# Second mixer of a two-layer decoder trunk: one transpose for both diagonal blocks of a triangular inverse, and five elementwise steps on other engines

## The chip, the cores and the metric

The kernel runs on one core of a Trainium2 chip. The core has TensorE (matmuls, written PE in the profile), VectorE (DVE), ScalarE (ACT), GpSimd (POOL), and SyncE (SP), which here only issues transfers. The metric is the device time of one execution in microseconds; a kernel's time is the median over its runs.

## What is computed

The reference is a trunk of two layers on a sequence of 512 tokens of width 1024. Each layer is a half feed-forward block, a token mixer, and another half feed-forward block, each followed by a layer norm:

```python
x = layer_norm(alpha * x + 0.5 * swiglu_ffn(x, ffn1_wi[l], ffn1_wo[l]), ...)
mix = even_mixer(x, ...) if l % 2 == 0 else odd_mixer(x, ...)
x = layer_norm(alpha * x + mix, ...)
x = layer_norm(alpha * x + 0.5 * swiglu_ffn(x, ffn2_wi[l], ffn2_wo[l]), ...)
```

The change touches the mixer of the second layer, `odd_mixer`. It runs two groups of heads side by side: RWKV-7 (8 heads of 64) and gated linear attention (GLA, 4 heads). The RWKV-7 part is a recurrence over time on a 64 x 64 state per head:

```python
def step(state, inp):
    r_t, w_t, k_t, v_t, kk_t, a_t = inp
    sa = jnp.einsum('bhij,bhj->bhi', state, -kk_t)
    state = (state * w_t[:, :, None, :] + sa[..., None] * (kk_t * a_t)[:, :, None, :]
             + v_t[..., None] * k_t[:, :, None, :])
    return state, jnp.einsum('bhij,bhj->bhi', state, r_t)
...
k = k * (1.0 + (a - 1.0) * k_a)
bonus = (jnp.sum(r * k * r_k, -1, keepdims=True) * v).reshape(B, S, RK_WIDTH)
return (y + bonus) * g
```

The GLA part ends in `head_norm(o, norm_g, None, GLA_NORM_EPS) * jax.nn.silu(og)`.

## The kernel before

All matrix products with weights are made as three matmuls each, from a high and a low part of both operands (lines 122, 123 and 126 for outputs with features on the partitions, 146 to 148 and 155 to 157 for outputs with tokens there). ScalarE makes the high part of each weight tile (line 98, `whi`), VectorE the low part (line 100, `wlo`).

In the second mixer, `odd` (line 555), the recurrence is cut into 8 chunks of 64 tokens. The 512 RWKV-7 channels are four feature tiles `ft` of 128 partitions, two heads each, and two tiles make a group, so there are two groups, each with 2 x 2 x 8 = 32 blocks of 64 x 64 (head and chunk). For each tile:

- `inputs(ft)` projects k, r and v and shifts them in time (line 599 on ScalarE, line 600 on VectorE).
- `keys(ft, ...)` (line 675) makes the decayed keys. Line 707 forms `fa = tha * KA + KAI` on VectorE, line 708 multiplies it by k, line 709 makes the decayed r, line 711 uses `fa`. Line 714 then overwrites r with r * RK * fa. Line 697 is a power on GpSimd for the norms of the keys.
- `bonus` (line 727) multiplies that r by a block of ones (line 729, `pb`).
- `scores` (line 733) makes two halves of four chunks each: matmuls of keys into `psc` (line 742), and the masked copy to `SC` on VectorE (line 744). Columns 64 to 127 of `SC`, rows 0 to 63, hold for each block a strictly upper triangular 64 x 64 matrix: two diagonal blocks of 32 x 32 (rows 0 to 31 with columns 64 to 95, rows 32 to 63 with columns 96 to 127), an upper block, and a lower block which is zero.
- `natural` (line 746) makes token-major copies.

`inverse(grp)` (line 770) inverts the two 32 x 32 diagonal blocks of all 32 matrices at once on VectorE. Line 778 transposes each diagonal block into `X`, one instruction on 32 partitions for each. Then 30 steps of two instructions each (lines 782 and 783, on 64 partitions) do the substitution, line 784 sets the diagonal, line 786 transposes the upper one of the results into `TQ`, which lies in the tile `WT`, and line 789 transposes both results back into `SC`, again one instruction for each block. `merge(grp)` (line 791) makes the off-diagonal block with matmuls: `pq` (line 800) needs line 786, its copies are line 802 (one half on ScalarE, one on VectorE); `px` (line 807) needs those and the lower right block of `SC`; its copies into `SC` are line 809; `pwt` and `pu` (line 822) read all of rows 0 to 63, columns 64 to 127. `chain(grp)` (line 830) then walks through the chunks.

The order at the top of the mixer is: `keys` and `scores` of the first group, its `inverse`, `gla_gates`, `natural`, `merge`; `keys` of tiles 2 and 3; `chain` of the first group; `scores`, `natural` and `inverse` of the second; its `merge` and `chain`. Line 917 to 959 and `gla` are the GLA part; in `gla_o`, line 957 to 959 make the gated output `og` (line 959 multiplies by the norm's weights, `ng`), which line 1030 reads much later.

Two things set the order of instructions. TensorE's waits are filled with projection work: `fill()` (line 646) puts as many steps of a waiting projection at its place as the list `FILL` (line 25, written out by hand) says, and ties them behind the last matmul before them. All else is ordered by a planner when the kernel is built: it simulates a timeline with its own estimate of each instruction's cost, and on each engine issues what is ready, in the order that comes out. So if instructions change engine, the planned order can change too, also that of instructions which the edit does not name.

Of the kernel before, what the change touches and what calls it, by code (L numbers as in the profile page):

```python
# [10 lines left out]
AF = mybir.ActivationFunctionType  # L11
ALU = mybir.AluOpType
# [19 lines left out]
class Net:  # L32
# [522 lines left out]
    def odd(self, l):  # L555
# [7 lines left out]
        with tc.tile_pool(name="od", bufs=1) as ep:  # L563
# [11 lines left out]
            IMU, KAI = 43, 56  # L575
# [17 lines left out]
            def col(i, n=P):  # L593
                return pc[:n, i:i + 1]
# [80 lines left out]
            def keys(ft, Dm, k, r, v):  # L675
# [30 lines left out]
                fa = slot("wk")  # L706
                V.tensor_scalar(out=fa, in0=tha, scalar1=col(KA + ft), scalar2=col(KAI + ft), op0=ALU.mult, op1=ALU.add)
                V.tensor_tensor(out=fa, in0=fa, in1=k, op=ALU.mult)
# [4 lines left out]

                V.scalar_tensor_tensor(out=r, in0=r, scalar=col(RK + ft), in1=fa, op0=ALU.mult, op1=ALU.mult)
                fill()
# [17 lines left out]
            def scores(f, grp, KRV, bk):  # L733
                KV, BK, SC, ZU, WT, R, _ = grp

                for c0 in (0, 4):
# [6 lines left out]
                    for par, p in enumerate(pp):  # L743
                        V.tensor_tensor(out=SC[:, 2 * f + par, c0:c0 + 4, :], in0=p.rearrange("p (c t) -> p c t", c=4), in1=m_rk.unsqueeze(1).broadcast_to([P, 4, P]), op=ALU.mult)

            def natural(f, grp, KRV, bk):
                KV, BK, SC, ZU, WT, R, _ = grp
# [22 lines left out]
            def inverse(grp):  # L770
# [4 lines left out]
                tmp = ZU[64:128].rearrange("p h c t -> p (h c t)")[:, 1024:1280]  # L775
                for z in range(2):
                    q = slice(32 * z, 32 * z + 32)
                    V.transpose(out=X[q], in_=SM[q, :, 64 + 32 * z:96 + 32 * z].rearrange("p m t -> p t m"))
                for j in range(1, 31):
# [6 lines left out]
                V.transpose(out=TQ[0:32].rearrange("p m j -> p j m"), in_=X[0:32].rearrange("p t j -> p j t"))  # L786
                for z in (1, 0):
                    q = slice(32 * z, 32 * z + 32)
                    V.transpose(out=SM[q, :, 64 + 32 * z:96 + 32 * z].rearrange("p m t -> p t m"), in_=X[q])

# [160 lines left out]
            def gla_o():  # L951
# [3 lines left out]
                for t in range(4):  # L955
                    o = gp.tile([P, S], F32, name=f"og{t}")
                    A.activation(o, acc[t], AF.Tanh, scale=0.5)
                    V.scalar_tensor_tensor(out=o, in0=o, scalar=1.0, in1=acc[t], op0=ALU.add, op1=ALU.mult)
                    V.tensor_tensor(out=o, in0=o, in1=ng, op=ALU.mult)
                    og.append(o)  # L960
# [304 lines left out]
```

## Time and profile before

| | |
|---|---|
| median of 3 runs | 2059.55 us (2056.95 to 2061.2) |
| the profiled execution | 2057.05 us, of which the span from first to last instruction is 2055.3 us |
| mean granted TensorE clock | 0.983 |
| VectorE busy | 1002.1 us, 1858 instructions |
| ScalarE busy | 687.5 us, 1206 instructions |
| GpSimd busy | 68.5 us, 128 instructions |
| the second mixer | about 1340 to 1660 us after the span's start |
| the two inverses, line 778 to line 789 | 1411.15 to 1468.40 and 1534.99 to 1576.99 |

How to read the profile's lines. In a timeline a line is: start and duration in us, engine, source line, operation, tile written <- tiles read, shape written <- shape read (partitions x elements per partition), how many instructions the line merges, and in brackets the idle time of that engine just before and who ended it. In a table of groups, a line is: source line, engine, operation, tiles, shapes and count, then total busy us and mean ns of one instruction, then the idle time before them and what ended it. In a table by stage, a line is the stage's start and end, its length, then each engine's busy time with its number of instructions, the granted TensorE clock as a share of full speed, the share in which the transfer engines were busy, and GB/s.

### The profile page before, as it was taken

Reading aid. Unit: us, or ns where it says so; the run is one execution under the profiler, and the core shown is the slowest. Engines: PE = TensorE matmul, PEld = TensorE weight load, DVE = VectorE, ACT = ScalarE, POOL = GpSimd, SP = SyncE. Lnnn points to the kernel's source line nnn. Section 1 sums busy time; section 2 is a strip of 40 time slices with the busy share of each in tenths; the row PEclk is TensorE's granted clock in tenths of the full one; section 3 lists DMA queues with packets and bytes.
Section 4 is the critical chain, followed back from the end, with each engine's and each line's share of the span. In section 5 each row is a group of like instructions: output and inputs, shape, how many; then the busy total and the mean of one; then the engine's idle time right before and its main releaser. Section 6 shows DMA issues by size and latency. Waiting matters only on the chain.

```text
span 2055.3 us, 26008 instructions
## 1 busy us (share of the span) xinstructions
PE 2014.7 (98%) x10485; PEld 1670.5 (81%) x10485; DVE 1002.1 (49%) x1858; ACT 687.5 (33%) x1206; POOL 68.5 (3%) x128
## 2 busy tenths in 40 slices
PE   9999999999999999999999999998898999999998
PEld 8888888977888888888888888886777688888886
DVE  4332333766783323336332333678758684323335
ACT  4331331556423322332332233255223334322330
POOL 0000000100010000000000000000010210000001
PEclk9999999999999999999999999998898999999999
DMA  5233332322233233332333333241113023333331
GB/s 176 93 102 113 103 93 82 107 92 62 66 100 113 92 102 114 101 95 72 113 92 103 113 98 97 86 140 40 59 31 114 1 74 119 95 97 118 94 102 62
DMA packets 56456, 191.42 MB, mean 93 GB/s; under 512 B 7488, under 2 KB 7952, under 8 KB 56336
## 3 DMA queue, kind: packets, MB, share of 16 engines
q1 hardware_dynamic: 56336, 189.77, 29.4%
q8 instruction: 82, 1.34, 0.3%
q14 instruction: 38, 0.31, 0.0%
HBM read 185.55 MB, written 4.19 MB: 92 GB/s over the span
## 4 chain that ended last, share of the span: by engine, by line
PE 90%; DVE 7%; ACT 1%; DMA 1%; issue 1%; POOL 0%; POOLq 0%; DVEq 0%; SPq 0%; ACTq 0%
PE pgu L122 16%; PE pgu L123 16%; PE pgu L126 16%; PE acc L157 8%; PE acc L155 8%; PE acc L156 8%; PE pout L155 1%; PE pout L156 1%; PE pout L157 1%; DVE wlo L100 1%; PE pj L122 1%; PE pj L123 1%; PE pj L126 1%; PE pst L168 1%; DVE ZU L782 1%; DVE ZU L783 1%
## 5 line engine op out<-in xcount | busy, mean ns | idle before, releaser
L100 DVE TENSOR_TENSOR wlo<-raw,whi 128x512 fp32r<-128x512 f32 x658 | 426.4, 686 | 549.6 <-ACT whi L98 513.2
L98 ACT ACTIVATE whi<-raw 128x512 fp32r<-128x512 f32 x661 | 379.6, 623 | 841.8 <-PE pgu L123 401.2
L122 PE MATMUL pgu<-xh,whi 128*128 128x512 f32 (+1 forms) x1568 | 563.1, 368 | 1.5 <-ACT whi L98 1.3
L123 PE MATMUL pgu<-xl,whi 128*128 128x512 f32 (+1 forms) x1568 | 564.0, 368 | 0.0
L126 PE MATMUL pgu<-xh,wlo 128*128 128x512 f32 (+1 forms) x1568 | 353.6, 367 | 0.0
L122 PEld LDWEIGHTS pgu<-xh,whi 128*128 128x128 f32 x1568 | 294.1, 188 | 50.4 <-ACT whi L98 1.5
L123 PEld LDWEIGHTS pgu<-xl,whi 128*128 128x128 f32 x1568 | 295.3, 189 | 48.6
L126 PEld LDWEIGHTS pgu<-xh,wlo 128*128 128x128 f32 x1568 | 275.8, 189 | 48.6
L155 PE MATMUL acc<-whi,hh 128*128 128x512 f32 x704 | 274.4, 390 | 0.0
L156 PE MATMUL acc<-whi,hl 128*128 128x512 f32 x704 | 274.2, 389 | 0.0
L157 PE MATMUL acc<-wlo,hh 128*128 128x512 f32 x704 | 272.3, 390 | 0.0
L233 DVE TENSOR_TENSOR sg<-sg,pgu 128x512 f32<-128x512 f32 (+1 forms) x96 | 61.6, 642 | 334.2 <-PE pgu L126 330.5
L156 PEld LDWEIGHTS acc<-whi,hl 128*128 128x128 f32 x704 | 132.2, 188 | 27.3
L157 PEld LDWEIGHTS acc<-wlo,hh 128*128 128x128 f32 x704 | 132.2, 188 | 27.2
L155 PEld LDWEIGHTS acc<-whi,hh 128*128 128x128 f32 x704 | 132.2, 188 | 27.0
L160 ACT ACTIVATE hh<-sg 128x512 fp32r<-128x512 f32 (+1 forms) x96 | 57.3, 597 | 120.9 <-DVE sg L233 120.9
L232 ACT ACTIVATE sg<-pgu 128x512 f32<-128x512 f32 (+1 forms) x96 | 53.7, 561 | 55.6 <-PE pgu L126 54.9
L160 ACT ACTIVATE xh<-pst 128x512 fp32r<-128x512 f32 x48 | 27.6, 598 | 108.5 <-PE pst L168 108.5
L122 PE MATMUL pj<-xh,whi 128*128 128x512 f32 (+2 forms) x184 | 63.5, 364 | 0.0
L190 POOL TENSOR_SCALAR rs<-mv 128x1 f32<-128x1 f32 x24 | 13.1, 547 | 1507.8 <-DVE mv L188 1507.8
L123 PE MATMUL pj<-xl,whi 128*128 128x512 f32 (+2 forms) x184 | 62.0, 354 | 0.0
L161 DVE TENSOR_TENSOR hl<-sg,hh 128x512 fp32r<-128x512 f32 (+1 forms) x96 | 61.5, 640 | 0.6 <-ACT hh L160 0.5
(336 smaller groups left out, 1968.6 us busy)
## 6 DMA issues: line engine op xcount, KB each, us to landing
raw<-ffn_wi SPq DMA_DIRECT2D x176, 512.0 KB, 3.5
raw<-ffn_wo SPq DMA_DIRECT2D x88, 512.0 KB, 3.5
raw<-od_krv SPq DMA_DIRECT2D x12, 512.0 KB, 3.5
raw<-ev_qk SPq DMA_DIRECT2D x8, 512.0 KB, 3.6
raw<-ev_rg SPq DMA_DIRECT2D x8, 512.0 KB, 3.5
raw<-ev_w_out SPq DMA_DIRECT2D x8, 512.0 KB, 3.5
raw<-od_w_out SPq DMA_DIRECT2D x8, 512.0 KB, 3.5
x<-x SPq DMA_DIRECT2D x4, 512.0 KB, 5.7
```

Source lines behind the costliest of these rows:

```text
L98: self.nc.scalar.activation(hi[:, sl], t[:, sl], AF.Copy)
L100: self.nc.vector.tensor_tensor(out=lo[:, sl], in0=t[:, sl], in1=hi[:, sl].bitcast(F32), op=ALU.subtract)
L122: mm(o, hi[:, kt, :n], self.xh[:, kt, t0:t1], start=kt == 0, stop=False)
L123: mm(o, hi[:, kt, :n], self.xl[:, kt, t0:t1], start=False, stop=lo is None and kt == 7)
L126: mm(o, lo[:, kt, :n], self.xh[:, kt, t0:t1], start=False, stop=kt == 7)
L155: mm(o, ah, hi[:, cs], start=first and i == 0, stop=False)
L156: mm(o, al, hi[:, cs], start=False, stop=False)
L157: mm(o, ah, lo[:, cs], start=False, stop=last and i == len(lhs) - 1)
L160: self.nc.scalar.activation(hi, src, AF.Copy)
L161: self.nc.vector.tensor_tensor(out=lo, in0=src, in1=hi.bitcast(F32), op=ALU.subtract)
L232: nc.scalar.activation(sg, pp[f, 0][:, t0:t1], AF.Silu)
L233: nc.vector.tensor_tensor(out=sg, in0=sg, in1=pp[u][:, t0:t1], op=ALU.mult)
```

## The change

The lower left 32 x 32 block of each matrix in `SC`, which is zero, serves as a place to put the lower right diagonal block under the upper left one, so that both stand in columns 64 to 95 of partitions 0 to 63. For this ScalarE copies the lower right block over in `scores`, after line 744. One transpose on 64 partitions then replaces the two of line 778, and one replaces the two of line 789. After that ScalarE copies the lower right result back to its own columns, and GpSimd sets the borrowed block to zero again.

Besides, `fa` of line 707 is made on ScalarE; line 714 becomes a scaling on ScalarE followed by a multiply on GpSimd; and the multiply of line 959 goes to GpSimd. `FILL` stays as it is.

```diff
@@ keys
                 fa = slot("wk")
-                V.tensor_scalar(out=fa, in0=tha, scalar1=col(KA + ft), scalar2=col(KAI + ft), op0=ALU.mult, op1=ALU.add)
+                A.activation(fa, tha, AF.Identity, scale=col(KA + ft), bias=col(KAI + ft))
                 V.tensor_tensor(out=fa, in0=fa, in1=k, op=ALU.mult)
...
-                V.scalar_tensor_tensor(out=r, in0=r, scalar=col(RK + ft), in1=fa, op0=ALU.mult, op1=ALU.mult)
+                A.activation(r, r, AF.Copy, scale=col(RK + ft))
+                G.tensor_tensor(out=r, in0=r, in1=fa, op=ALU.mult)
@@ scores
                         V.tensor_tensor(out=SC[:, 2 * f + par, c0:c0 + 4, :], ...)
+
+                    s = SC[32:64, 2 * f:2 * f + 2, c0:c0 + 4, :]
+                    A.activation(s[:, :, :, 64:96], s[:, :, :, 96:128], AF.Copy)
@@ inverse
-                for z in range(2):
-                    q = slice(32 * z, 32 * z + 32)
-                    V.transpose(out=X[q], in_=SM[q, :, 64 + 32 * z:96 + 32 * z].rearrange("p m t -> p t m"))
+                V.transpose(out=X, in_=SM[0:64, :, 64:96].rearrange("p m t -> p t m"))
...
                 V.transpose(out=TQ[0:32].rearrange("p m j -> p j m"), in_=X[0:32].rearrange("p t j -> p j t"))
-                for z in (1, 0):
-                    q = slice(32 * z, 32 * z + 32)
-                    V.transpose(out=SM[q, :, 64 + 32 * z:96 + 32 * z].rearrange("p m t -> p t m"), in_=X[q])
+                V.transpose(out=SM[0:64, :, 64:96].rearrange("p m t -> p t m"), in_=X)
+                A.activation(SM[32:64, :, 96:128], SM[32:64, :, 64:96], AF.Copy)
+                G.memset(SM[32:64, :, 64:96], 0.0)
@@ gla_o
-                    V.tensor_tensor(out=o, in0=o, in1=ng, op=ALU.mult)
+                    G.tensor_tensor(out=o, in0=o, in1=ng, op=ALU.mult)
```

## The prediction

> **What bounds the kernel now.** I read the page first: engine totals, then the chain that ended last.
>
> ```profile
> PE 2014.7 (98%) x10485; PEld 1670.5 (81%) x10485; DVE 1002.1 (49%) x1858; ACT 687.5 (33%) x1206; POOL 68.5 (3%) x128
> PE 90%; DVE 7%; ACT 1%; DMA 1%; issue 1%; POOL 0%; POOLq 0%; DVEq 0%; SPq 0%; ACTq 0%
> ```
>
> TensorE sets the end nearly everywhere; VectorE owns 7% of the chain. An edit that takes work from VectorE can pay only where TensorE waits for VectorE. So I cut the second mixer into stages (busy time per engine; the figure behind POOL's is the granted TensorE clock) and asked who waits longest for whom.
>
> ```profile
> core 0: us, PE busy (x) PEld busy (x) DVE busy (x) ACT busy (x) POOL busy (x), PEclk, DMA share, GB/s
> 1391.00:1431.00 40.00, 33.14 (x181) 22.22 (x179) 35.12 (x61) 23.24 (x37) 2.96 (x5) 0.86 0.12 40
> 1431.00:1463.00 32.00, 32.00 (x168) 26.17 (x166) 29.21 (x67) 11.68 (x20) 1.11 (x1) 0.96 0.26 76
> 1463.00:1485.00 22.00, 16.54 (x283) 13.73 (x282) 13.57 (x16) 5.20 (x9) 0.53 (x1) 0.69 0.15 48
> ...
> 1568.00:1588.00 20.00, 12.88 (x180) 10.01 (x180) 12.75 (x16) 3.64 (x7) 0.00 (x0) 0.66 0.15 55
> ```
> ```profile
> PE pq L800 <- DVE WT L786: 6.2, 2, 4.8
> ```
>
> Two ends of an inverse stand out. At the first (1463 to 1485) TensorE is idle 22.00 - 16.54 = 5.46 us, at the second (1568 to 1588) 20.00 - 12.88 = 7.12 us; the longest wait of the kernel is TensorE's for L786, the transpose that ends the inverse. Both stages also show a clock of 0.69 and 0.66. In rows of 2 us the clock is full or about half (one with 0.51 stands further down), so a mean of 0.69 is half clock for 22 x 0.31 / 0.5 = 13.6 us, and 0.66 for 20 x 0.34 / 0.5 = 13.6 us. Between them, 1431 to 1463, TensorE has no gap: there a quicker VectorE buys nothing by itself. From 1391 to 1431 TensorE is idle 6.86 us in small waits.
>
> The timeline of VectorE around the two inverses:
>
> ```profile
> 1391.47 1.29 DVE L100 TENSOR_TENSOR wlo<-raw,whi 128x512 fp32r<-128x512 f32 x2 [5.03 <-PE pj L126]
> ...
> 1417.07 0.75 DVE L714 SCALAR_TENSOR_TENSOR kr<-kr,pc,wk 128x512 f32<-128x512 f32 x1
> ...
> 1434.37 0.43 DVE L966 TENSOR_SCALAR cst<-cst 128x512 f32<-128x512 f32 x1 [0.92 <-DMA cst<-gla_norm_g]
> ...
> 1462.47 1.98 DVE L786 STREAM_TRANSPOSE WT<-ZU 32x1024 f32<-32x1024 f32 x1
> 1464.49 3.92 DVE L789 STREAM_TRANSPOSE SC<-ZU 32x1024 f32<-32x1024 f32 x2
> ...
> 1469.22 0.69 DVE L802 COPY WT<-pq 32x512 f32<-32x512 f32 x1
> ...
> 1474.27 0.69 DVE L809 COPY SC<-px 32x512 f32<-32x512 f32 x1
> ...
> 1571.28 1.90 DVE L786 STREAM_TRANSPOSE WT<-ZU 32x1024 f32<-32x1024 f32 x1
> 1573.20 3.79 DVE L789 STREAM_TRANSPOSE SC<-ZU 32x1024 f32<-32x1024 f32 x2
> 1577.02 0.69 DVE L802 COPY WT<-pq 32x512 f32<-32x512 f32 x1
> ```
>
> and TensorE's matmuls that stood behind it (in brackets: how long, and for whom):
>
> ```profile
> 1395.33 1.33 PE L908 MATMUL pl<-ga,gw 80*128 80x512 f32 x2 [1.86 <-DVE wk L721]
> ...
> 1422.27 1.02 PE L729 MATMUL pb<-kr,cst 128*128 128x512 f32 x2
> ...
> 1464.60 1.20 PE L800 MATMUL pq<-WT,SC 32*32 32x32 f32 x64 [1.37 <-DVE WT L786]
> ...
> 1475.01 1.76 PE L822 MATMUL pwt<-SC,KV 64*64 64x64 f32 x28 [2.70 <-DVE SC L809]
> ...
> 1573.32 1.81 PE L800 MATMUL pq<-WT,SC 32*32 32x32 f32 x64 [4.79 <-DVE WT L786]
> ...
> 1577.77 1.91 PE L807 MATMUL px<-SC,WT 32*32 32x32 f32 x62 [1.66 <-DVE WT L802]
> ```
>
> The reading: after L786 the two L789 transposes hold up the copy L802, which px needs, and in the first merge a queue of other VectorE work holds up L809, which pwt needs.
>
> **The change, part by part.** Durations of what is moved, with ScalarE's rows for the same shapes:
>
> ```profile
> L778 DVE STREAM_TRANSPOSE ZU<-SC 32x1024 f32<-32x1024 f32 x4 | 7.9, 1986 | 0.1
> L714 DVE SCALAR_TENSOR_TENSOR kr<-kr,pc,wk 128x512 f32<-128x512 f32 x4 | 3.0, 747 | 0.1
> L959 DVE TENSOR_TENSOR og<-og,cst 128x512 f32<-128x512 f32 x4 | 2.8, 689 | 0.1
> L707 DVE TENSOR_SCALAR wk<-wk,pc 128x512 f32<-128x512 f32 x4 | 2.1, 536 | 0.0
> ```
> ```profile
> L599 ACT ACTIVATE kr<-pj,pc 128x512 f32<-128x512 f32 x12 | 8.1, 681 | 3.9 <-PE pj L126 3.9
> L802 ACT COPY WT<-pq 32x512 f32<-32x512 f32 x2 | 1.2, 577 | 7.3 <-PE pq L800 7.3
> ```
>
> *Transposes.* Four L778 become two on 64 partitions, four L789 likewise. No row shows a 64-partition transpose. Its ends are the time of one 32-partition transpose (1.99 us) and of two (3.97 us). I take 1.99: each partition still carries 1024 elements. So 2.0 us go ahead of each inverse and 1.9 us behind it. In exchange ScalarE gets eight mask copies of 256 elements (at most the 0.58 us of the 512-element copy) and two copies of 1024 elements (about twice 0.58, 1.15 us), and GpSimd two memsets.
>
> *Elementwise.* L707 (4 x 0.54 us) goes to ScalarE at about 0.68 each (L599's form). L714 (4 x 0.75 us) becomes a ScalarE scaling (0.68) and a GpSimd multiply. L959 (4 x 0.69 us) becomes a GpSimd multiply. In all VectorE loses 3.97 + 3.8 + 2.1 + 3.0 + 2.8 = 15.7 us; what of it lies on the path is the question.
>
> *GpSimd's price.* The nearest rows, and two that show how GpSimd and VectorE meet:
>
> ```profile
> L697 POOL TENSOR_TENSOR nrm<-nrm,expo 128x8 f32<-128x8 f32 x4 | 6.7, 1681 | 73.5 <-DVE nrm L696 73.5
> ...
> L329 POOL MEMSET wbd<- 128x1024 f32 x1 | 1.0, 956 | 4.4 <-DVE x L196 4.4
> ```
> ```profile
> 1408.57 0.75 POOL L932 COPY Dg<-E 128x8 f32<-128x8 f32 x1 [3.12 <-ACT E L930]
> 1410.13 0.19 POOL L932 COPY Dg<-E 128x8 f32<-128x8 f32 x1 [0.81 <-ACT E L930]
> ```
> ```profile
> 1408.12 1.21 DVE L920 TENSOR_TENSOR_SCAN ga<-cst,wk 128x512 f32<-128x512 f32 x1
> ```
>
> A multiply of 512 elements lies between half the 1024-element memset (0.48) and the longest row of this stage (1.68); I take 1.1, the middle. The same GpSimd copy took 0.19 us, but 0.75 us when VectorE's scan was running, and ended with it (1409.32 against 1409.33). So GpSimd waits out a VectorE instruction that reads two tensors from SBUF. The Trainium skill, "SBUF — State Buffer", section "SBUF: two separate sides", says that the two share a port pair as an exclusive lock, and that a GpSimd instruction which reads SBUF likewise keeps such a VectorE instruction out for its whole length. The trace agrees with the first half; no row here can show the second, since GpSimd's reads are tiny. I therefore charge each GpSimd multiply in a stretch where VectorE is packed with between 0 and 1.1 us of VectorE time, and take 1.1: there the move loses 0.4 us instead of winning 0.7. The skill's "GPSIMD Engine Reference", section "Performance versus the Vector engine", gives 4497 ns for a two-input operation on 2048 elements, from which I estimate 1.12 us here; by that figure the sum would be unchanged. The memset (about 1.0 us) runs behind the ScalarE copy while px and its copies run; if these didn't cover it, it would cost pwt up to 1.0 us.
>
> *First pair of keys.* For ft 0 and 1 the moved steps lie before 1391, where VectorE then sits idle 5.03 us waiting for TensorE: nothing gained.
>
> *First inverse.* Between L778 and L786 there go one transpose (2.0), L714 twice (1.5) and L707 once (0.54), 4.0 us; the two GpSimd multiplies give back 2.2. L786 ends 1.9 us earlier, and pq's 1.37 us are gone. Behind it 1.96 us of L789 go too, so L809 comes 1.9 + 1.96 = 3.9 us earlier. TensorE's 5.46 idle us there shrink by **3.9**; with no lock by all 5.46. What is late next: TensorE's own packed matmuls before 1463.
>
> *Clock at the first inverse.* Of 13.6 us at half clock TensorE is busy about 10.2 (all but 0.7 and 2.70), so full clock would be worth 5.1. About 1.5 us of idle remain. In this trace an idle 1.86 us (L908) was followed by half clock, shown by the row below, but only for some 4 us. So I take **2.0** of the 5.1; ends 0 and 5.1.
>
> ```profile
> 1396.00:1398.00 2.00, 2.00 (x5) 1.61 (x6) 1.77 (x3) 2.00 (x4) 0.00 (x0) 0.51 0.00 0
> ```
>
> *Second inverse.* Ahead of L786: 2.0 us of transpose, less 0.5 for the last mask copy, which now stands between L744 and the transpose, and 0.7 for the L959 that ran just before L786: pq starts **2.2** earlier, 2.6 of the 4.79 stay. Then px started 4.45 us after pq, behind two L789. Now the transpose takes 1.9, ScalarE's copy 1.15, and ScalarE's WT copy behind it 0.58: 3.6 us, so **0.9** more. The remaining gap is above 1.86, so I leave the half clock.
>
> *ScalarE's new work.* From 1391 to 1431 it is busy 23.24 of 40 us and gets two mask copies, one L707 and one scaling more, some 2.3 us, in a strictly ordered queue whose results TensorE awaits in small waits. I charge **+1.0** (0 to 2.3).
>
> Sum: -3.9 - 2.0 - 2.2 - 0.9 + 1.0 = -8.0 us. The profiled execution took 2057.05 us (2055.3 of span, 1.75 around it), so it would take 2049.0. It lies 2.5 us under the median of 2059.55 of the three runs; the median would be 2051.5.
>
> **Rivals.**
>
> *Clock kept.* The Trainium skill, "TensorE: Matmul & The Clock Gate", Part 1, says that the clock is halved after an idle window of about 3.4 us. By that rule 2.6 us left at the second inverse would not halve it. Against it stands the 1.86 us wait that did. As a mechanism of this kernel: second stage, 13.6 us at half clock of which 11.3 busy, worth 5.6; at the first 5.1 instead of 2.0. Then the sum is -8.0 - 5.6 - 3.1 = -16.7: 2043.
>
> *Nothing won.* A 64-partition transpose takes 3.97 us. Then the first inverse has 2.05 us of elementwise work less and 2.2 of lock more (+0.15), the second wins L959's 0.7 and pays 0.5 for the mask copy, px comes 3.8 + 1.15 + 0.58 = 5.5 us after L786 instead of 4.45 (+1.1), and ScalarE costs 1.0: +2, 2061.5. It is also the case where the planner, whose estimates now differ, places the work so that the waits merely move. Speaks against: a VectorE row is priced by elements per partition wherever this trace lets me compare (L802 on 32 and L100 on 128 partitions, 512 elements, 0.69 and 1.29 / 2).
>
> *Slower: GpSimd's multiply starves.* From 1415 to 1433 VectorE runs without a gap, mostly two-tensor instructions; its first gap is the 0.92 us before L966 at 1434.37. If the multiply of ft 2, ready at about 1417.5, gets in only there, pb at 1422.27 starts at 1434.6, 12.3 us late, with all of TensorE's queue behind it. The inverse goes on meanwhile, so TensorE's 5.46 us are swallowed, half clock after so long a gap costs 4 or more, and 3.1 come back at the second inverse: 12.3 - 5.5 + 4 - 3.1 = +7.7, 2067. It decides once the multiply ends later than 1422.27 + 8 = 1430. Against it: GpSimd's copy got in right after one VectorE instruction, inside a packed stretch.
>
> **How the numbers follow.** Forecast 0.54, clock kept 0.15, nothing won 0.17, slower 0.14. A measurement of this kernel tells about 0.2% (4.1 us) from no change. The forecast with its bounds (-5 to -11) and the clock rival are faster, 0.69, and I give 0.01 of "nothing won" to that side: 0.70 faster, 0.16 same, 0.14 slower. The range runs from 2040 (clock kept, no lock and no cost on ScalarE: -16.7 - 1.5 - 1.0 = -19.2) to 2062, just past "nothing won", and leaves out the starving case. The forecast's own range is 2048 to 2055.
>
> **What would show it.** Right: two transposes at about 2.0 us and 64x1024 in L778's place per kernel; pq's waits at 0 and about 2.6; pwt's 2.70 gone; a clock mean above 0.69 in the first stage. Wrong: transposes near 4 us; GpSimd multiplies far above 1.1 us or VectorE rows stretched beside them; new TensorE waits for ScalarE between 1391 and 1431, or for the r multiply at pb.

## The result and the profile after

The changed kernel took 2042.95 us in the median of five executions (2040.22 to 2049.03), against 2059.45 us of the kernel before (2056.95 to 2061.2): a ratio of 0.9927, 95% interval 0.991 to 0.9943, or 15 us (12 to 19). Twelve more executions in a later series gave 2048.01 us (2040.37 to 2055.2), against 2059.32 us of before in that series: 0.9942 (0.9921 to 0.9963), or 12 us (8 to 16). The forecast was 8 us, to 2051.5. The profiled execution took 2041.09 us (span 2039.3).

First the page of after, totals and chain:

```profile
PE 2005.6 (98%) x10485; PEld 1664.0 (82%) x10485; DVE 989.9 (49%) x1842; ACT 698.4 (34%) x1224; POOL 81.0 (4%) x138
PE 91%; DVE 5%; ACT 2%; DMA 1%; issue 1%; POOL 0%; POOLq 0%; DVEq 0%; SPq 0%; ACTq 0%
```

TensorE's idle time fell from 2055.3 - 2014.7 = 40.6 us to 2039.3 - 2005.6 = 33.7 us. The other 9.1 us are busy time, with the same 10485 matmuls: these ran at a higher clock. VectorE's share of the chain went from 7% to 5%, ScalarE's from 1% to 2%. Then the stages of the mixer, as in the prediction, each beginning about as far ahead of its pq:

```profile
1391.00:1431.00 40.00, 34.03 (x184) 23.53 (x183) 36.12 (x65) 26.18 (x43) 3.49 (x6) 0.85 0.14 41
1431.00:1459.00 28.00, 28.00 (x152) 23.08 (x151) 25.39 (x55) 12.45 (x21) 1.47 (x1) 0.97 0.27 83
1459.00:1481.00 22.00, 18.69 (x289) 14.85 (x287) 11.93 (x18) 6.26 (x10) 2.58 (x2) 0.75 0.16 50
1559.00:1579.00 20.00, 16.06 (x230) 12.79 (x228) 11.25 (x18) 7.87 (x14) 4.21 (x4) 0.74 0.29 98
```

The first pq came 4.4 us earlier (1460.18 against 1464.60), and TensorE is idle for 3.31 us there (5.46 before), at the second for 3.94 us (7.12). The clock is 0.75 and 0.74 (0.69 and 0.66 before), not full. Who waits for whom, from after's list of waits (sum, count, longest):

```profile
PE pi L720 <- ACT wk L718: 2.3, 2, 2.0
PE pq L802 <- DVE WT L788: 2.2, 1, 2.2
PE pn L694 <- ACT wk L690: 1.9, 1, 1.9
PE px L809 <- ACT SC L790: 1.7, 1, 1.7
```

pq's 6.2 us are down to 2.2, all of it at the second inverse. pi waits for ScalarE, which it did not before. px waits for ScalarE's copy of the lower right result (L790); before, it waited 1.9 us for VectorE's copy of pq and 0.7 us for ScalarE's. The prices of the new instructions, from after's groups (total us, mean ns):

```profile
L780 DVE STREAM_TRANSPOSE ZU<-SC 64x1024 f32<-64x1024 f32 x2 | 4.0, 1983 | 0.7 <-ACT SC L748 0.7
L789 DVE STREAM_TRANSPOSE SC<-ZU 64x1024 f32<-64x1024 f32 x2 | 3.8, 1894 | 0.0
L707 ACT ACTIVATE wk<-wk,pc 128x512 f32<-128x512 f32 x4 | 3.2, 806 | 0.0
L748 ACT ACTIVATE SC<-SC 32x256 f32<-32x256 f32 x8 | 3.3, 416 | 7.4 <-DVE SC L745 7.3
L715 POOL TENSOR_TENSOR kr<-kr,wk 128x512 f32<-128x512 f32 x4 | 6.2, 1558 | 60.3 <-DVE wk L708 30.9 <-ACT kr L714 29.4
L961 POOL TENSOR_TENSOR og<-og,cst 128x512 f32<-128x512 f32 x4 | 4.4, 1092 | 39.6 <-DVE og L960 39.6
```

64 partitions take the time of 32 in the transpose. The last two lines are the same kind of GpSimd multiply. L715 ran beside VectorE instructions that read two tensors: 1.74 and 1.73 us ahead of the first inverse, 1.29 and 1.47 us within it, 1558 ns in the mean. The four L961 took 1.09 us each; none of them started while such an instruction was running.

### Where the time went, stage by stage

Cutting the mixer at TensorE's own marks shows more than the stages above. The marks are the first matmuls of pl, of the first pq, of psa in the first chain, of the second pq, of psa in the second chain, and the last psa. Lengths in us, from the view by stages of each kernel's profile; the experiments' rows are used further down, and the dummy matmuls of two of them do not count as pq.

| kernel | ratio to before (95%) | pl to pq | pq to psa | psa to 2nd pq | 2nd pq to psa | 2nd chain | its clock |
|---|---|---|---|---|---|---|---|
| before | 1 | 69.27 | 17.22 | 91.50 | 20.79 | 41.50 | 0.88 |
| after | 0.9927 (0.991-0.9943) | 64.89 | 19.10 | 84.75 | 20.70 | 34.92 | 1.00 |
| after again | 0.9942 (0.9921-0.9963) | 64.72 | 20.21 | 88.81 | 21.36 | 34.90 | 1.00 |
| transposes only | 0.9934 (0.9908-0.996) | 67.83 | 15.40 | 88.92 | 21.25 | 34.89 | 1.00 |
| moves only | 0.9989 (0.9967-1.0012) | 66.90 | 16.34 | 84.69 | 22.01 | 44.71 | 0.73 |
| r on VectorE | 0.9951 (0.9927-0.9974) | 67.53 | 17.71 | 85.01 | 20.69 | 46.56 | 0.71 |
| before, gap filled | 1.0016 (0.9994-1.0038) | 69.74 | 17.21 | 87.04 | 23.06 | 45.29 | 0.74 |
| before, one swap | 0.9982 (0.9968-0.9996) | 70.93 | 17.16 | 92.43 | 21.39 | 36.60 | 1.00 |
| r on VectorE, swap | 0.9951 (0.9931-0.997) | 67.29 | 17.90 | 84.79 | 20.70 | 34.05 | 1.00 |
| zeroing on VectorE | 0.995 (0.9928-0.9972) | 66.16 | 20.23 | 88.78 | 21.32 | 34.91 | 1.00 |
| after, gaps filled | 0.9946 (0.9927-0.9964) | 66.22 | 20.21 | 88.74 | 21.42 | 34.91 | 1.00 |
| after, px direct | 0.9933 (0.9906-0.996) | 66.01 | 15.15 | 89.99 | 21.56 | 34.90 | 1.00 |
| front half only, swap | 0.9946 (0.9925-0.9966) | 66.12 | 17.34 | 84.84 | 23.20 | 34.66 | 1.00 |
| transposes, px direct | 0.9927 (0.99-0.9955) | 67.91 | 15.32 | 89.00 | 21.29 | 34.92 | 1.00 |

Two stages differ by more than 6 us between before and the first profile of after. From the first psa to the second pq it is 91.50 - 84.75 = 6.75 us, of which the second profile of after shows 2.7. In the second chain it is 41.50 - 34.92 = 6.6 us, in both profiles; the change does not touch this stage, and the prediction did not price it. The row of each, before and then after:

```profile
1594.11:1635.61 41.50, 37.41 (x322) 27.47 (x322) 27.80 (x111) 11.96 (x31) 10.18 (x25) 0.88 0.01 2
```
```profile
1584.73:1619.65 34.92, 31.76 (x307) 23.71 (x306) 27.49 (x110) 12.45 (x32) 10.67 (x26) 1.00 0.01 2
```

The chain of before runs at a clock of 0.88, that of after at full clock. The cause stands in VectorE's timeline. Before, chunk 1 of the second chain:

```profile
1600.95 0.69 DVE L1030 TENSOR_TENSOR kr<-kr,og 128x512 f32<-128x512 f32 x1 [1.88 <-ACT kr L883]
1601.56 0.41 DVE L841 TENSOR_TENSOR KV<-psa,ZU 64x256 f32<-64x256 f32 x1
```

And TensorE in the same kernel:

```profile
1599.69 0.65 PE L1006 MATMUL pkv<-kr,kn 64*64 64x128 f32 x8
1602.03 1.22 PE L847 MATMUL pst<-KV,BK 128*128 128x128 f32 x4 [1.68 <-DVE KV L841]
```

The multiply L1030 (GLA output times gate) waits 1.88 us for ScalarE at the head of VectorE's queue, and L841, which the chain needs, stands behind it although its psa has been written by 1599.76. TensorE waits 1.68 us, and its matmuls run at half clock behind the wait (1.22 us for four that take 0.71 at full clock). The half clock begins at 1600.82, inside this wait; the 3.41 us before that hold 1.41 us of idle time, 0.94 of a wait for L852 and 0.47 of this one. In after the planner put the two the other way round:

```profile
1588.46 0.42 DVE L843 TENSOR_TENSOR KV<-psa,ZU 64x256 f32<-64x256 f32 x1 [0.72 <-PE psa L842]
1589.05 0.42 DVE L1011 TENSOR_TENSOR Sg<-pkv,Sg 128x256 f32<-128x256 f32 x1 [0.18 <-PE pkv L1008]
1589.51 0.42 DVE L1012 TENSOR_TENSOR Sg<-Sg,Dg 128x256 f32<-128x256 f32 x1
1589.86 0.68 DVE L1032 TENSOR_TENSOR kr<-kr,og 128x512 f32<-128x512 f32 x1
```

### The profile page after: what moved, and what is told of

It reads as the page before. It is cut to its first block, busy times and chain, and to the rows that moved or that the text cites. A ratio compares the mean times of both kernels' runs of the same rounds, so it can differ in the third digit from the quotient of the medians.

```text
span 2039.3 us, 26025 instructions
## 1 busy us (share of the span) xinstructions
PE 2005.6 (98%) x10485; PEld 1664.0 (82%) x10485; DVE 989.9 (49%) x1842; ACT 698.4 (34%) x1224; POOL 81.0 (4%) x138
## 3 DMA queue, kind: packets, MB, share of 16 engines
q8 instruction: 82, 1.34, 0.3%
## 4 chain that ended last, share of the span: by engine, by line
PE 91%; DVE 5%; ACT 2%; DMA 1%; issue 1%; POOL 0%; POOLq 0%; DVEq 0%; SPq 0%; ACTq 0%
PE pgu L122 16%; PE pgu L123 16%; PE pgu L126 16%; PE acc L155 8%; PE acc L157 8%; PE acc L156 8%; PE pout L155 1%; PE pout L156 1%; PE pout L157 1%; DVE wlo L100 1%; PE pst L168 1%; PE pv L146 1%; PE pj L122 1%; PE po L146 1%; PE pv L148 1%
## 5 line engine op out<-in xcount | busy, mean ns | idle before, releaser
L100 DVE TENSOR_TENSOR wlo<-raw,whi 128x512 fp32r<-128x512 f32 x658 | 426.7, 687 | 545.8 <-ACT whi L98 510.6
L157 PEld LDWEIGHTS acc<-wlo,hh 128*128 128x128 f32 x704 | 132.2, 188 | 27.3
```

The source lines that it names most:

```text
L100: self.nc.vector.tensor_tensor(out=lo[:, sl], in0=t[:, sl], in1=hi[:, sl].bitcast(F32), op=ALU.subtract)
L157: mm(o, ah, lo[:, cs], start=False, stop=last and i == len(lhs) - 1)
```

## The experiments

Three theories went in. W: the change won the waits at the two inverses and nothing else. K: those waits also start stretches at half clock, and shortening them is the rest. P: the rest is the planner's new order in the chains.

### The parts of the change, one without the other

What the title and the expectations call five elementwise steps are three lines of the kernel (L707, L714, L959), twelve instructions in all.

Transposes only (after, with the elementwise steps back on VectorE):

```diff
-                A.activation(fa, tha, AF.Identity, scale=col(KA + ft), bias=col(KAI + ft))
+                V.tensor_scalar(out=fa, in0=tha, ...)
-                A.activation(r, r, AF.Copy, scale=col(RK + ft))
-                G.tensor_tensor(out=r, in0=r, in1=fa, op=ALU.mult)
+                V.scalar_tensor_tensor(out=r, in0=r, scalar=col(RK + ft), in1=fa, ...)
-                    G.tensor_tensor(out=o, in0=o, in1=ng, op=ALU.mult)
+                    V.tensor_tensor(out=o, in0=o, in1=ng, op=ALU.mult)
```

> The change with its elementwise part undone: L707, L714 and the gating multiply are back on VectorE; merged transposes, mask copies, copy back and zeroing stay. Three theories. W (waits only): the change won the TensorE waits at the two inverse ends and nothing else; the transposes are 2.0 us of each wait, so about -5 us against before: 2054. K (waits and clock): TensorE's waits also start stretches at about half clock in steps of 3.4 us; in the profile of after these sum to 37.5 us in the mixer against 61.4 before, worth about 9 us on top of 7 us of waits; with the transposes alone most waits shrink, so -8 to -14 us: 2045 to 2051. P (the planner's other order of instructions won the chains): the order follows the VectorE load, and without the elementwise moves the chains fall back to before's time (53 and 41 us from first pwt to the end of each chain): -5 us or less.

Measured: 2045.97 us (2038.89 to 2048.09), 0.9934 (0.9908 to 0.996). This is all that the whole change brings, within the intervals. W's 2054 is too slow, and K's range (2045 to 2051) holds it. P as it was put is wrong too: the second chain did not fall back (34.89 us), because the planner has L842 ahead of L1031 here as well. The order does not follow the amount of VectorE work.

Moves only (before, with the same lines changed the other way round):

> Before with only the elementwise moves: L707 and L714 to ScalarE and GpSimd, the gating multiply to GpSimd; transposes as before. W: VectorE loses 2.05 us ahead of the first inverse and pays about 2.1 us of lock for two GpSimd multiplies, and 0.7 us ahead of the second: -1 us against before, 2058. K: the waits of 4.8 and 2.7 us stay nearly whole, so the half clock stays too: -3 to +1 us, 2056 to 2060. P: the chains are won by the new order, which the moves bring about: -5 to -10 us, 2049 to 2054.

Measured: 2055.94 us (2050.07 to 2063.37), 0.9989 (0.9967 to 1.0012): no difference that can be told. In the profile, pl to the first psa is 83.24 us against 86.49, 3.2 us shorter, and the second chain is 3.2 us longer, with the multiply ahead of L842 (TensorE's wait 1.30 us). The profiled execution was the fastest of its ten (2050.07): from the first psa to the second pq it is 6.8 us shorter than before's and lacks a stretch of 10.24 us at half clock, which comes and goes in one kernel, as shown below.

r back on VectorE (after, with only L714 as one instruction again):

```diff
-                A.activation(r, r, AF.Copy, scale=col(RK + ft))
-                G.tensor_tensor(out=r, in0=r, in1=fa, op=ALU.mult)
+                V.scalar_tensor_tensor(out=r, in0=r, scalar=col(RK + ft), in1=fa, op0=ALU.mult, op1=ALU.mult)
```

> The change with L714 alone back on VectorE as one instruction: no GpSimd multiply at r. The profile of after shows VectorE rows of 0.27 and 0.36 us stretched to 1.37 and 1.34 beside two of these multiplies. If that exclusion costs what the prediction charged, the move of r was worth nothing or less: VectorE gets 2 x 0.75 us of work back and loses 2 x 1.0 us of blocking before the first inverse: within 2 us of after, 2041 to 2045, and no VectorE row of L785 above 0.5 us. If the move of r is itself what made the first inverse earlier: 1.5 us or more slower than after, 2045 to 2048.

Measured: 2049.41 us (2044.66 to 2056.7), 0.9951 (0.9927 to 0.9974). No row of the substitution is above 0.41 us, so the stretched rows of after were the GpSimd multiplies' doing. These rows in after's timeline:

```profile
1414.49 0.27 DVE L784 TENSOR_TENSOR ZU<-ZU 64x108 f32<-64x108 f32 x1
1414.80 1.37 DVE L785 TENSOR_TENSOR ZU<-ZU 64x108 f32<-64x108 f32 x1
```
```profile
1414.75 1.29 POOL L715 TENSOR_TENSOR kr<-kr,wk 128x512 f32<-128x512 f32 x1 [3.74 <-ACT kr L714]
```

Two VectorE instructions on the same shape, 0.27 and 1.37 us; the second stands still until GpSimd's multiply is through (1416.04). But the time came out above the expected 2041 to 2045, and the table says where: the first inverse is as in after to 1.3 us (85.24 against 83.99), and the second chain took 46.56 us at a clock of 0.71. This kernel has the multiply ahead of L842 again:

```profile
1588.72:1635.28 46.56, 43.19 (x307) 31.78 (x306) 27.04 (x109) 11.97 (x31) 10.22 (x25) 0.71 0.01 1
```

### A wait filled with work that nobody needs

Before, with 14 dummy matmuls of 512 columns ahead of the second pq, into pq's own tile, which pq overwrites:

```diff
                 p = self.psum("pq", "C")
+                if yg_at:
+                    with tc.issue_after(self.last(mybir.EngineType.PE)):
+                        for _ in range(NDUM):
+                            T.matmul(p, self.zero[:, :P], self.zero, start=True, stop=True)
+                yg_at.append(1)
```

> Before, with 14 dummy matmuls of 512 columns in the second merge, issued right behind TensorE's last matmul ahead of pq, into a tile that pq overwrites: some 3 of the 4.79 us in which TensorE waits for L786 are filled with work that no result needs, and nothing else is edited. W and P: no wait becomes shorter for the results and the order stays, so 0 us against before, 2059 (up to 1 us slower if the dummies run past L786). K: the stretch of 13.65 us at half clock that follows this wait goes or shrinks, and perhaps the 10.24 us one behind it: -3 to -10 us, 2049 to 2056, with a clock near 0.9 or more from pq to pwt against 0.67.

Measured: 2059.95 us (2055.95 to 2065.46), 1.0016 (0.9994 to 1.0038). K's gain did not come. pq's wait went from 4.79 to 1.68 us, but px now waits 0.80 and 2.25 us where it waited 0.67 and 1.66, and the stretch at half clock stayed 13.65 us long. The gap was not filled whole: the 3.41 us ahead of that stretch still hold 2.21 us of idle time. So this run does not tell what a filled gap would do to the clock; the run with both gaps filled, further down, comes closer.

### One pair of instructions swapped

Before, with the first multiply of L1030 tied behind the addition of chunk 1 (`kv_add` collects the instructions of line 841). In the planned order of all engines these two VectorE instructions change places, and nothing else:

```diff
                                     in1=ZU[0:64, :, c, :].rearrange(...), op=ALU.add)
+                    kv_add.append(self.last(mybir.EngineType.DVE))
...
-                    V.tensor_tensor(out=yg[t], in0=yg[t], in1=og[t], op=ALU.mult)
+                    with tc.issue_after(kv_add[9] if t == 0 else kv_add[0]):
+                        V.tensor_tensor(out=yg[t], in0=yg[t], in1=og[t], op=ALU.mult)
```

> Before, with one thing changed: the first multiply of L1030 on VectorE is tied behind the addition L841 of chunk 1 of the second chain. In the planned order these two change places on VectorE, and no other instruction of any engine moves. In the profile of before, L1030 waits 1.88 us for ScalarE at the head of VectorE's queue while L841 behind it is ready, TensorE's pst waits 1.68 us for L841, and 10.24 us at half clock begin there; after and the run with the transposes alone have L841 first, no such wait and no half clock in this chain. If the planner's order is what won the second chain (theory P): the wait and the half clock go, -6 us or more against before, 2050 to 2054. If the half clock comes with the merge before it and falls where the phase lets it (theory K): the wait alone, -1.5 us, 2057 to 2058.

Measured: 2053.96 us (2049.91 to 2056.61), 0.9982 (0.9968 to 0.9996), that is 3.7 us (0.8 to 6.6). VectorE in this kernel (L1033 is before's L1030), and its second chain:

```profile
1601.62 0.42 DVE L841 TENSOR_TENSOR KV<-psa,ZU 64x256 f32<-64x256 f32 x1 [0.72 <-PE psa L840]
1602.78 0.69 DVE L1033 TENSOR_TENSOR kr<-kr,og 128x512 f32<-128x512 f32 x1 [0.74 <-ACT kr L884]
```
```profile
1595.94:1632.54 36.60, 33.56 (x322) 24.71 (x322) 27.66 (x111) 11.96 (x31) 10.20 (x25) 1.00 0.01 2
```

The wait of pst is gone and the chain runs at full clock, as P said. The gain in the medians lies between K's 1.5 us and P's 6; its interval excludes zero, but neither of them.

The same swap in the kernel with r on VectorE:

> The same one swap on VectorE in the change with r back on VectorE, whose profile shows 27.3 us at half clock from this place on (wait 1.31 us for L842). P: -5 to -10 us against that kernel's 2049, so 2040 to 2044, the time of after or better, and the move of r to GpSimd is worth nothing by itself. K: -1.3 us, about 2048.

Measured: 2045.82 us (2042.07 to 2049.01), 0.9951 (0.9931 to 0.997). The chain does what P says, 34.05 us at full clock against 46.56:

```profile
1590.34:1624.39 34.05, 31.99 (x306) 23.82 (x306) 26.72 (x109) 11.96 (x31) 10.21 (x25) 1.00 0.01 2
```

The times do not show it: both ratios are 0.9951, the medians lie 3.6 us apart. The profiled execution without the swap was the slowest of its ten (2056.7, mean clock 0.982). Six of the ten have a mean clock of 0.987 or 0.988, as the profile with the swap has (0.987), and four have 0.982 to 0.985. So the long stretch is in four of them at most, as far as the mean clock tells. What both swaps show is the wait and the clock of this chain; of the 4.9 us between the profiles of the first pair the times confirm 0.8 to 6.6, of the 12.5 us of the second pair none.

The mean clock is on record for every execution, and (1 - clock) x span is the clock time that it lost, an upper bound on what full clock would win. In the mean of each series, the swap in before lost 30.6 us against 36.5, for a mean time 4.7 us shorter. After (again) lost 27.3 us against 36.5, for 11.2 us. So the clock can account for all that the swap won, and for up to 9.2 of the 11.2 us of the whole change.

### The zeroing, and both gaps filled

After, with the zeroing of the borrowed block on VectorE (`V.memset` in the place of `G.memset`):

> The change with the zeroing of the borrowed block on VectorE and not on GpSimd. In the profile of after the zeroing (0.94 us) stands ahead of the power L697 on GpSimd, whose result TensorE's pi awaits for 2.03 us through ScalarE; the prediction took the zeroing to be covered. If this is a cost of the change: pi's wait shrinks below 1.3 us and the time is 0.5 to 3 us under after's 2043, 2040 to 2042.5. If it is covered by what waits there anyway (px stands behind pi and waits for its own operands): within 1 us of after, 2042 to 2044, the idle time moving from pi to px or pwt.

Measured: 2048.44 us (2044.49 to 2050.31), 0.995 (0.9928 to 0.9972). pi's wait did not shrink (2.40 us): the zeroing was not what made it. The power on GpSimd that pi's chain needs takes 1.64 us here in both kernels, and in after it began 0.23 us behind its input (1463.04 against 1462.81). So the prediction's "covered" was right for this instruction, and VectorE is no better place for it: the time is that of after again, above both expected ranges.

What made pi wait stands in VectorE's order. L696, 0.16 us long, starts the chain that runs over GpSimd (L697) and ScalarE (L718 in after) to pi. Before, it stood ahead of the transpose L786, which began at 1462.47:

```profile
1461.59 0.16 DVE L696 TENSOR_SCALAR nrm<-pn 128x8 f32<-128x8 f32 x1
```

In after it stands behind both transposes and three other instructions, although the first transpose starts 5.5 us earlier:

```profile
1456.92 2.06 DVE L788 STREAM_TRANSPOSE WT<-ZU 32x1024 f32<-32x1024 f32 x1
1462.65 0.16 DVE L696 TENSOR_SCALAR nrm<-pn 128x8 f32<-128x8 f32 x1
1463.04 1.64 POOL L697 TENSOR_TENSOR nrm<-nrm,expo 128x8 f32<-128x8 f32 x1
1464.71 0.63 ACT L718 ACTIVATE wk<-nrm 128x512 f32<-128x512 f32 x1 [2.21 <-POOL nrm L697]
1465.40 0.66 PE L720 MATMUL pi<-ident,wk 128*128 128x128 f32 x4 [2.03 <-ACT wk L718]
```

In the two kernels with both transposes merged and the elementwise steps on VectorE, L696 stands ahead of the transposes and pi does not wait. No run moved L696 alone.

After, with dummies in both gaps of the second merge, 9 ahead of pq and 7 ahead of px:

> After, with 9 dummy matmuls of 512 columns ahead of pq and 7 ahead of px in the second merge, which fill the 2.20 and 1.75 us that TensorE waits there; the other instructions keep their order but for one copy on ScalarE. If the 10.24 us at half clock in the second merge come from these waits: they go or shrink to one step of 3.4 us, and the merge is 3 to 5 us shorter, 2038 to 2041. If pq and px themselves, which use 32 by 32 of TensorE's 128 by 128 and then stand between waits, count as too little work whatever fills the gaps: the half clock stays, and the time is that of after, 2042 to 2045.

Measured: 2045.64 us (2038.05 to 2055.02), 0.9946 (0.9927 to 0.9964). The half clock behind the second pq shrank from 10.24 to 6.8 us, one step of 3.41 us less and not gone, and the merge is no shorter (21.42 us against 20.70 and 21.36). The step won is worth nothing that can be seen; that pq, px and pwt are paced by the copies between them would explain it, and was not tried by itself.

### After again, and what the swaps leave

> The changed kernel once more, for a second profile and more times. In profiles of seven kernels so far the waits of TensorE repeat within 0.1 us where the order of instructions is the same, but the stretches at half clock differ: the 1.29 us wait for L854 in the first chain is followed by 10.24 us at half clock in four profiles and by none in five. If that hangs on the phase of a 3.4 us step and not on the kernel, this second profile may show that stretch although the first did not, with the same waits; the median then comes out above the first 2043, at 2043 to 2047. If the change itself removed it, the profile shows no half clock between 1490 and 1560 again and the median stays at 2041 to 2044.

Measured: 2048.01 us (2040.37 to 2055.2), 0.9942 (0.9921 to 0.9963), a little above the 2043 to 2047 expected if it is phase. The order and the waits of the chains are the same as in the first profile, and in the first chain there is now a stretch at half clock. Both profiles have the same wait there. (Of the ten profiles before this one, five have the stretch behind this wait and five have not.) The first profile of after in steps of 3.41 us (the half-clock stretches of a profile begin and end on such a grid):

```profile
1507.61:1511.02 3.41, 2.54 (x15) 1.80 (x13) 1.86 (x6) 1.43 (x4) 1.06 (x2) 1.00 0.01 2
1511.02:1514.44 3.42, 3.01 (x22) 2.33 (x22) 1.14 (x5) 0.00 (x0) 0.00 (x0) 1.00 0.00 0
1514.44:1517.85 3.41, 3.41 (x34) 2.72 (x33) 2.46 (x10) 1.42 (x3) 0.00 (x0) 1.00 0.02 5
```

The second profile:

```profile
1510.63:1514.04 3.41, 3.32 (x20) 2.43 (x19) 1.08 (x4) 1.43 (x4) 1.66 (x4) 1.00 0.17 67
1514.04:1517.45 3.41, 2.21 (x17) 1.86 (x18) 1.71 (x8) 0.00 (x0) 0.00 (x0) 1.00 0.00 0
1517.45:1520.87 3.42, 3.42 (x21) 2.54 (x21) 0.90 (x4) 0.00 (x0) 0.00 (x0) 0.50 0.00 0
```

And the wait itself, in the first and in the second:

```profile
1511.43 0.29 PE L842 MATMUL psa<-St,WT 128*64 128x128 f32 x1 [1.29 <-DVE St L854]
```
```profile
1515.24 0.29 PE L842 MATMUL psa<-St,WT 128*64 128x128 f32 x1 [1.29 <-DVE St L854]
```

In the first, the 1.29 us are cut by the grid into 3.41 - 2.54 = 0.87 and 0.41 us, and the clock stays full. In the second, 1.20 us fall into one step, and the next step is at half clock, and two more after it. The stage from psa to the second pq is 4.1 us longer for it (88.81 against 84.75), in the same kernel. So 4.1 of the 16.0 us between the first two profiles were chance.

After with px reading columns 64 to 95, where the merged transpose leaves the result, with ScalarE's copy and GpSimd's zeroing moved behind pq's copies and px:

```diff
-                A.activation(SM[32:64, :, 96:128], SM[32:64, :, 64:96], AF.Copy)
-                G.memset(SM[32:64, :, 64:96], 0.0)
...
+                with tc.issue_after(self.last(mybir.EngineType.Activation)):
+                    A.activation(SM[32:64, :, 96:128], SM[32:64, :, 64:96], AF.Copy)
...
-                    T.matmul(p[q, ...], TQ[32:64, m, :], SM[32:64, m, 96:128], start=True, stop=True)
+                    T.matmul(p[q, ...], TQ[32:64, m, :], SM[32:64, m, 64:96], start=True, stop=True)
+                G.memset(SM[32:64, :, 64:96], 0.0)
```

> The change with px reading the lower right result at columns 64 to 95, where the merged transpose leaves it; ScalarE's copy back stands behind its copy of pq, and GpSimd's zeroing behind px. L1032 is tied as in the runs with the swap, which leaves after's order as it is. In after TensorE waits 1.75 us for ScalarE's copy ahead of the second px. If that copy is what px waits for: the wait falls to about 0.9 us (WT copies alone), pwt comes 0 to 0.3 us later behind px than now (zeroing 0.95 against the copies' 0.69 us), and the time is 0.5 to 2 us under after's. If the WT copies set px anyway, or the zeroing now holds up pwt: within 0.5 us of after, or up to 1 us slower.

Measured: 2046.06 us (2039.55 to 2048.53), 0.9933 (0.9906 to 0.996). At the second merge px waits 0.67 and 0.42 us where it waited 1.75, and the merge is not shorter (21.56 us). At the first, TensorE takes px ahead of pi, pi waits 0.52 us, and pl to the first psa is 81.16 us against 83.99 and 84.93. The times show no gain that can be told from after.

Before with the front half of the merged transposes alone (mask copies, one transpose for the two of L778) and the swap:

> Before with the front half of the merged transposes alone: mask copies and one transpose for the two of L778, the borrowed block zeroed behind it; L789 stays two instructions, and all elementwise steps stay on VectorE. The first multiply of L1030 is tied as in the one-swap run, so that the second chain is not part of the difference. By the prediction's terms the front half is 2.0 us ahead of each pq: pq's waits 1.37 and 4.79 become 0 and about 3, and 2.0 + 2.0 us less 0.6 for the mask copies on ScalarE is -3.4 us against the one-swap run: 2050.5. The back half (behind L786) would then account for the rest between this and the transposes alone. If TensorE's waits are only half of what an earlier pq wins (clock), -5 to -8: 2046 to 2049.

Measured: 2044.42 us (2041.87 to 2056.07), 0.9946 (0.9925 to 0.9966), 11 us under before and 7 under the swap alone. The second pq waits 2.20 us, as in after, but px behind the two L789 waits 0.71 and 2.98 us, and that merge takes 23.20 us. The front half brings most of what the transposes bring; the back half's share is below what these intervals resolve.

The transposes alone with px direct:

> The transposes alone with px reading columns 64 to 95 as in the other kernel of this call, and the elementwise steps on VectorE. Against that kernel it tells what the five elementwise moves are worth once the order in the second chain is the same: by the prediction's terms 0.4 x 2 us lost to the lock, 0.54 won by L707 ahead of the first inverse, 0.7 by the gating multiply ahead of the second, less ScalarE's extra work: 0 to 1 us, so the two within 1.5 us of each other. If the moves are worth what the first medians suggest (2043 against 2046): 3 us slower than that kernel.

Measured: 2043.09 us (2040.39 to 2050.98), 0.9927 (0.99 to 0.9955), against 0.9933 with the elementwise moves. The elementwise moves are worth nothing that can be seen, which is near the 0 to 1 us of the prediction's terms. No version here beats after by more than the intervals; this one equals it without the moves.

## Why the prediction was right, and where it was not

The side and the range were right, and the size was too small by 4 to 7 us: the forecast's own range, 2048 to 2055, misses the first median and just holds the second. That the whole range holds both is in part luck, since the largest gain that both profiles show was in no term, and a term of 2.0 us came to nothing. By its own steps:

**The prices.** "Each partition still carries 1024 elements", so 1.99 us: measured 1.98 and 1.89. That settled the rival "nothing won", whose 3.97 us did not appear. The mask copies took 0.42 us (at most 0.58), L707, with a column each for scale and bias, 0.81 us on ScalarE (0.68 taken), the gating multiply 1.09 us on GpSimd (1.1). No TensorE wait for GpSimd's r multiply shows, so the starving rival fell too.

**The lock.** The charge of up to 1.1 us per GpSimd multiply in a packed stretch was borne out: two steps of the first inverse went from 0.27 to 1.37 us and from 0.36 to 1.34. The Trainium skill, "SBUF — State Buffer", section "SBUF: two separate sides", has this rule in both directions, and this trace now agrees with both.

**The second inverse.** pq was to keep 2.6 us of wait and start 2.2 us earlier: it kept 2.20, and from the first psa to it 88.81 us passed (after again) against 91.50, 2.7 less; these two profiles both have the stretch at half clock in the first chain. The 0.9 us for px were not seen: its wait went from 2.33 to 1.75 us, and the stage from 20.79 to 20.70 and 21.36.

**The first inverse.** The terms -3.9, -2.0 and +1.0 were to give -4.9 us from pl to the first psa. Measured: 86.49 to 83.99 and 84.93, so -2.5 and -1.6. The step that failed is the clock: "I take 2.0 of the 5.1" measured 0. Before has one stretch of 13.65 us at half clock there, both profiles of after have 3.41 + 10.24 = 13.65. With the rival "clock kept" it is the same: its 2043 is near the first median by luck, as the half clock it was to remove is there in all but a step (10.24 of 13.65 us at the second merge). The idle time fell by 3.0 and 1.6 us, for 2.9 forecast net of ScalarE, as pwt's 2.70 us became 0.89 and 1.09 but pi got 2.03 and 2.40. In the first profile pi's wait lies in one step of 3.41 us, and 3.41 us at half clock follow; then pwt's waits, 1.28 us in one step, and 10.24 us follow. So the half clock came back behind a wait that the prediction did not have.

L786 was to end 1.9 us earlier (4.0 less 2.2 is 1.8); its counterpart ended 5.5 us earlier, at 1458.98. The terms themselves came out about as priced. But the first transpose also began 0.9 us earlier, with L707 of that tile (0.53 us) gone from in front of it, which the prediction did not count, and the planner put 2.9 us of other VectorE work outside the stretch: one L708 ahead of it, L938, two L100 and L696 behind it. L696 is the one that made pi wait. The +1.0 us for ScalarE did not show where it was charged: from 1391 to 1431 TensorE's idle time fell from 6.86 to 5.97 us, and only pn waits longer for ScalarE there (1.88 us against 1.30).

**The second chain.** The missing term. The prediction had the planner's changed order only as a way in which "the waits merely move"; here it removed one, 1.68 us of TensorE and the half clock behind it. In the profiles it is 6.6 us, more than any term of the sum; alone, by the swap, 0.8 to 6.6 us.

With the second profile of after the account closes: -1.6 (first inverse), -2.7 (second pq), +0.6 (its merge), -6.6 (second chain) are -10.3 us. pl itself came 3.3 us later than in before, ahead of these stages and not in the first profile of the same kernel, and the span is 2055.3 - 10.3 + 3.3 = 2048.3.

The theories: W is refuted by the transposes alone. K holds for the chains, where the grid decides, and is not shown for the merges, where filling the waits took away one step at half clock and won nothing. P is shown for the second chain, by all profiles: in the four kernels with the multiply ahead (before, moves only, r on VectorE, gap filled) the chain's clock is 0.71 to 0.88, in the ten with the addition ahead it is 1.00. The front half is worth 7 us in the times although pq's two waits fell by 0.9 and 2.6 only: in the mean it lost 26.8 us to the clock, the swap alone 30.6. Open: which waits those 4 us go back to, and in how many executions each long stretch at half clock comes, as the record has one mean clock for each.

## What to carry to other kernels

When a planner orders instructions, compare the order of both kernels at every in-order queue before trusting a sum: an instruction that waits for another engine at the head of VectorE's queue may cost more than the edit wins, and a tie of one line mends it. Before pricing a wait's effect on the clock, look where it falls in the grid of 3.41 us and in how many profiles it does. And take work off VectorE only where TensorE waits for it: the transposes ahead of pq paid, the elementwise moves did not.

## What the runs showed of the hardware

The clock. In steps of 3.41 us, over the second mixer of all 14 profiles (about 1343 to 1655 us): of 945 steps at full clock in which TensorE was idle for less than 0.8 us, 4 were followed by a step at half clock; of the 15 with 0.8 to 0.9 us, 3; of 57 with 0.9 to 1.8 us, 40; of 44 with more, 42. So a single wait of 1.2 us can halve the clock for 10 us if it lies within one step, and the same wait does nothing if the grid cuts it. Once halved, the clock can stay so although TensorE is never idle: of the 27.31 us at half clock in r on VectorE, eight steps, the last seven have no idle time. The Trainium skill, "TensorE: Matmul & The Clock Gate", Part 1, has the free-running window of 3413 ns, which agrees with the steps; its rule that a whole idle window (some 3.4 us) is what halves the clock does not: here 1.20 us of idle did. The spread of one kernel's executions goes with the clock too: over before's 31 in the first series the mean clock goes from 0.987 in the fastest (2048.84 us) to 0.972 in the slowest (2073.15), which is 27 and 58 us of clock time lost, and over all 31 the time and the loss have a correlation of 0.92.

Two engines that hold each other up: a VectorE step of 0.27 us that reads two tensors took 1.37 us beside a GpSimd multiply, and that kind of multiply took 1.29 to 1.74 us among such steps where it takes 1.09 without them.
